# First stage of a conditioned decoder block on one core: both token halves in one loop over eight feature blocks, the modulation 128 columns at a time, three column blocks multiplied behind the loop

## The chip, the core and the metric

The kernel runs on one core of one Trainium2 chip. The metric is the time of one execution on the device in microseconds (us). The engines of the core have these names: PE multiplies matrices (its weight loads are shown as PEld), DVE and ACT work element by element on tiles, POOL is the general engine, SP issues most of the DMA transfers. Every engine works through its own list of instructions in order, so an instruction that waits holds up all that stand behind it in that list, DMA issues included.

## The reference

The block takes 1024 tokens of 1024 features and a conditioning vector `c`. All is float32. Only the first lines bear on the change; the rest (state-space branch, attention, merge, feed-forward) is the same in both kernels.

```python
cond = jax.nn.silu(c)
mod = (cond @ w_ada[l] + b_ada[l])[:, None, :]
sh1, sc1, g1, sh2, sc2, g2 = jnp.split(mod, N_ADA, axis=-1)
h = modulate(rmsnorm(x, norm1_g[l]), sh1, sc1)        # h * (1 + sc1) + sh1
proj = h @ w_in[l]
u, q, k, v, gate_a, gate_b = jnp.split(proj, IN_SPLITS, axis=-1)
y_a = s5_branch(u, ...) @ w_a[l]
y_b = stick_breaking_attention(q, k, v) @ w_b[l]
```

The first stage computes `sh1` and `sc1` (columns 0 to 2047 of `cond @ w_ada`), normalizes and modulates the tokens, keeps `h` turned (features on the partitions) for all later products, and multiplies it with the first 512 columns of `w_in`, which gives `u`, the input of the state-space branch (called S5 here).

## The kernel before

Every float32 product is made as three matmuls of rounded parts: an operand is split into an upper part `h` (a cast, by ACT) and a lower part `l` (the operand less its upper part, by DVE), and upper times upper, upper times lower and lower times upper are added in PSUM. `PRODUCTS` lists the three pairs.

`start` (L563) is the first stage. There the order on every engine is the order of the code (`manual_schedule`). The 1024 tokens are two halves of 512, h = 0 and 1, with four tiles `x` of 128 tokens each; the 1024 features are eight blocks k of 128. The steps are:

- `load(h)` fetches four tiles `x`; `square`, `rstd` and `scale` normalize them in place (the squares' sums are split between ACT and DVE, and so is the scaling).
- `ada_load(g)` fetches the columns of `w_ada` for two feature blocks (256 columns of shift, 256 of scale, four tiles of 512 KB each), g = 0 to 3. `ada_products(g)` multiplies them with `cond` (16 matmuls), ACT copies the result to the tile `acc`, and `ada_sums(g)` adds it up over the partitions with four narrow matmuls. DVE makes `mod` and `G` from it.
- `u_load(a)` fetches the weights of `u` for the feature blocks 2a and 2a+1, and `u_split(a)` makes their upper and lower parts. The four pairs of tiles are called `wh`/`wl` (a = 0 and a = 1, two buffers), `wgh`/`wgl` (a = 2) and `u3h`/`u3l` (a = 3).
- `turn(h, k)` transposes feature block k of a half on PE, and `modulate(h, k)` makes the upper and lower parts of `h` from it, with the steps `hf` (ACT or DVE), cast (ACT, L657) and difference (DVE, L658). They lie in tiles `pa` for half 0 and `pb` for half 1, and are kept for the whole first part of the kernel.
- `product(h, ks, ms)` multiplies feature blocks ks with the column blocks ms (four of 128 columns each), accumulating over all eight k in one PSUM bank for each column block; `store(h, m)` copies a bank to SBUF and writes it to `uD` in memory.
- `idle(n)` issues transposes whose result nobody reads.

First comes a loop over g with half 0 alone, whose second half-tiles `x` are loaded at g = 0 and squared at g = 2; then half 1 in a loop over k. Pieces of `s5.steps` (coefficients of the state-space branch, small DVE operations), `s5.load`, `s5.turned` and `s5.matrices` are called in between.

What follows `start` is put in order by the scheduler: the runs of the S5 branch and `v_proj` (L776), the value projection, whose weights come through `weight` (L438) in the ring of tiles `wh`/`wl`, `wh`/`wl`, `wgh`/`wgl`. So the first two sets of `v_proj` take the tiles in which the weights of `u` for a = 0 (`wh`/`wl`) and a = 2 (`wgh`/`wgl`) lay: a cast into one waits for the last matmul that reads it. A matmul of `v_proj` has 256 columns, and 24 of them on `wh`/`wl` and 24 on `wgh`/`wgl` belong to two token tiles. PE's order of both programs is the same from about 1,300 instructions on.

Of the kernel before, what the change touches and what calls it, by code (L numbers as in the profile page):

```python
# [9 lines left out]
F32 = mybir.dt.float32  # L10
# [18 lines left out]
class S5:  # L29
# [23 lines left out]
    def vexp(self, dst, x, tmp):  # L53
# [8 lines left out]
        v.scalar_tensor_tensor(f, n, -LN2L, f, ALU.mult, ALU.add)  # L62
        v.tensor_scalar(q, f, 1.0 / math.factorial(8), None, ALU.mult)
# [19 lines left out]
    def steps(self):  # L83
# [5 lines left out]
        self.vexp(dt, ldt, tmp)  # L89
# [3 lines left out]
        self.vexp(r, ar, tmp)  # L93
# [336 lines left out]
class Block:  # L430
# [123 lines left out]
    def small(self, const, pp):  # L554

        nc, rows = self.nc, self.rows_
        nc.vector.tensor_copy(rows[0:16].rearrange("p (a b) -> p a b", a=2), self.ld.unsqueeze(2).broadcast_to([16, 2, 64]))
        self.cols = const.tile([P, P], F32, name="cols")
        ps = pp.tile([P, 512], F32, name="mm")
        nc.tensor.transpose(ps[:, 0:P], rows, self.ident)  # L560
        nc.vector.tensor_copy(self.cols, ps[:, 0:P])

    def start(self, const, up, s5p):  # L563
# [5 lines left out]
        w_v = i["w_ada"].rearrange("o (p k) n -> (o p) k n", k=KT)  # L569
        u_v = i["w_in"][0].rearrange("(k p) n -> p k n", p=P)  # L570
        self.hT = [[self.PA.tile([P, 2, 512], F32R, name="pa") for _ in range(KT)], []]
        with self.pool("s0", 1, side="right") as sp, self.pool("s0a", 1, side="right") as ap, self.pool("s5t", 1, side="right") as st, \
                self.pool("s0p", 1, PSUM) as pp, self.pool("s0t", 2, PSUM) as tp, self.pool("s0x", 1, PSUM) as xp, self.pool("s0m", 2, PSUM) as mp, \
                self.tc.manual_schedule(engines={E.PE, E.Activation, E.DVE, E.Pool, E.SP}):
            x = [None] * KT
            ps = pp.tile([P, 2, KT], F32, name="adap")
# [3 lines left out]

# [13 lines left out]
            def u_split(a):  # L594
                w, h, l = us[a]
                nc.scalar.copy(h, w)
                nc.vector.tensor_tensor(l, w, h.bitcast(F32), ALU.subtract)
                ws[a] = self.w3((h, l), 512)

            def ada_load(g):  # L600
                ada[g] = []
                for q in range(2):
                    for a in range(2):
                        w = self.PB.tile([P, 4, 256], F32, name="pb")
                        n = 1024 * q + 256 * g
                        self.last_ada = nc.sync.dma_start(out=w, in_=w_v[:, 4 * a:4 * a + 4, n:n + 256])
                        ada[g].append(w)

            def ada_products(g):
                t = xp.tile([P, 512], F32, name="mm")  # L610
                for q in range(2):
                    for k in range(KT):
                        self.ada_mm(t[:, 256 * q:256 * q + 256], k, ada[g][2 * q + k // 4][:, k % 4])
                ada[g] = ap.tile([P, 512], F32, name="acc", bufs=2)
                nc.scalar.copy(ada[g], t)

            def ada_sums(g):
                for q in range(2):
                    for j in range(2):
                        c = 256 * q + P * j  # L620
                        nc.tensor.matmul(ps[:, q, 2 * g + j:2 * g + j + 1], lhsT=ada[g][:, c:c + P], rhs=self.ones[:, 0:1], start=True, stop=True)
                s = slice(2 * g, 2 * g + 2)
                b = self.cols[:, 64:80].rearrange("p (q k) -> p q k", q=2)
                nc.vector.tensor_tensor(mod[:, :, s], ps[:, :, s], b[:, :, s], ALU.add)
                nc.vector.scalar_tensor_tensor(G[:, s], mod[:, 1, s], 1.0, self.cols[:, 48 + 2 * g:50 + 2 * g], ALU.add, ALU.mult)

            def square(t, act):
                sq = ap.tile([P, 1024], F32, name="sqa" if act else "sqv")
# [5 lines left out]
            def scale(r, t):  # L634
                if t % 4 == 0:
                    nc.scalar.mul(x[t], x[t], r[:, t % 4:t % 4 + 1])
                else:
                    nc.vector.tensor_scalar(x[t], x[t], r[:, t % 4:t % 4 + 1], None, ALU.mult)

            def idle(n):  # L640
                for _ in range(n):
                    nc.tensor.transpose(acc[3][:, 0:P], self.ident, self.ident)
# [6 lines left out]
            def modulate(h, k):  # L649
                t, q = self.hT[h][k], turned[h, k]  # L650
                f = ap.tile([P, 512], F32, name="hf", bufs=2)
                if h == 0 and k % 2 == 0:
                    nc.scalar.activation(t[:, 0], q, AF.Identity, bias=mod[:, 0, k:k + 1], scale=G[:, k:k + 1])
                    nc.vector.tensor_scalar(f, q, G[:, k:k + 1], mod[:, 0, k:k + 1], ALU.mult, ALU.add)
                else:
                    nc.scalar.activation(f, q, AF.Identity, bias=mod[:, 0, k:k + 1], scale=G[:, k:k + 1])
                    nc.scalar.copy(t[:, 0], f)  # L657
                nc.vector.tensor_tensor(t[:, 1], f, t[:, 0].bitcast(F32), ALU.subtract)  # L658

            def product(h, ks, ms):  # L660
                for k in ks:
                    for m in ms:
                        for n, (a, b) in enumerate(((0, 0), (1, 0), (0, 1))):
                            nc.tensor.matmul(acc[m], lhsT=ws[k // 2][a][:, k % 2, P * m:P * m + P], rhs=self.hT[h][k][:, b], start=k + n == 0, stop=k + n == KT + 1)  # L664

            def store(h, m):
                u = up.tile([P, 8, 64], F32, name="us", bufs=4)
                self.upin = (nc.vector.tensor_copy if m % 2 > h else nc.scalar.copy)(u, acc[m].rearrange("p (c j) -> p j c", j=8))
# [10 lines left out]
            acc = [(self.mm, mp)[m // 2].tile([P, 512], F32, name="mm") for m in range(4)]  # L679
# [4 lines left out]
            for t in range(4):  # L684
                scale(r, t)
            turn(0, 0)
            turn(0, 1)
            u_split(0)
            self.small(const, xp)
            ada_products(0)  # L690
# [3 lines left out]
            idle(4)  # L694
            ada_sums(0)
            idle(9)
            for g in range(4):
                k = 2 * g
                modulate(0, k)
# [918 lines left out]
```

## Time and profile before

| what | value |
|---|---|
| median of 3 runs | 1432.78 us (1430.53 to 1435.14) |
| the profiled execution | 1436.13 us |
| its span, first to last instruction | 1434.4 us |
| clock granted to PE, mean | 0.996 |
| PE / DVE / ACT / POOL busy | 98% / 75% / 45% / 36% |
| last matmul of the first stage ends | 93.40 us from the span's start |

The span is cut into what each engine did; a row of the time line gives the start, the length, the engine, the line of the kernel and the tiles (written <- read), and in brackets how long the engine stood still before it and which instruction it waited for. A matmul of 512 columns is recorded with 0.39 to 0.40 us, though the next one starts 0.23 us after it: they overlap in PE's pipeline. The chain of waits is the path that ended last, followed back from the end.

### The profile page before, as it was taken

What the parts mean: (1) busy time and instruction counts of PE and PEld (TensorE: products, weight loads), DVE (VectorE), ACT (ScalarE), POOL (GpSimd) and SP (SyncE); (2) the same over time, 40 slices, a digit from 0 to 9 for tenths busy, and PEclk for the clock granted to TensorE, in tenths of its full rate; (3) what the DMA queues carried; (4) which work ended last, traced back from release to release, by engine and by line L of the source; (5) the groups of instructions that cost most, each with busy time, mean ns of one, the idle gap of its engine ahead of it and who ended that gap; (6) DMA issues with size and microseconds to landing.
All of it is one profiled execution on the core that took longest, in us unless ns stands there. A gap on an engine that the chain in (4) does not pass through costs nothing.

```text
span 1434.4 us, 18472 instructions
## 1 busy us (share of the span) xinstructions
PE 1408.1 (98%) x6821; PEld 1121.3 (78%) x6821; DVE 1078.4 (75%) x1388; ACT 639.9 (45%) x852; POOL 514.5 (36%) x288
## 2 busy tenths in 40 slices
PE   8899999998999999999999999999999999999997
PEld 6689888887666666668888888888888888788886
DVE  5679985656897989877824697877667667799896
ACT  4433324423777776774328442332323233433335
POOL 1020000102101111104400017776767666699394
PEclk9999999999999999999999999999999999999999
DMA  9656667299011112217533234444444359899722
GB/s 338 170 136 178 161 161 213 69 334 310 16 52 52 44 30 81 66 38 240 190 121 118 68 91 152 167 139 162 140 162 138 117 198 386 287 370 364 253 81 117
DMA packets 193274, 233.41 MB, mean 163 GB/s; under 512 B 29468, under 2 KB 128864, under 8 KB 193184
## 3 DMA queue, kind: packets, MB, share of 16 engines
q1 hardware_dynamic: 184048, 224.70, 47.8%
q10 hardware_dynamic: 8912, 7.48, 1.9%
q8 instruction: 54, 0.88, 0.3%
q14 instruction: 36, 0.29, 0.1%
q0 software_dynamic: 224, 0.05, 0.0%
HBM read 162.85 MB, written 68.16 MB: 161 GB/s over the span
## 4 chain that ended last, share of the span: by engine, by line
PE 80%; DVE 9%; DMA 5%; ACT 3%; issue 2%; POOL 1%; SPq 0%; ACTq 0%; POOLq 0%; DVEq 0%
PE tq L1308 12%; PE wo L1308 6%; PE tq L1429 6%; PE mm L1308 6%; PE mx L838 5%; PE mm L838 5%; PE mm L767 4%; PE mm L1429 3%; PE mx L767 3%; PE wo L1429 3%; PE acc L838 2%; PE wo L1145 2%; PE mm L1145 2%; PE mm L664 2%; PE z L838 2%
## 5 line engine op out<-in xcount | busy, mean ns | idle before, releaser
L475 POOL TENSOR_TENSOR ws<-wb 128x1024 f32<-128x1024 f32 x24 | 60.6, 2526 | 171.4 <-DVE wl L478 142.7
L459 POOL TENSOR_TENSOR wl<-ws,wh 128x1024 fp32r<-128x1024 f32 x12 | 31.4, 2616 | 151.4 <-ACT wh L456 150.9
L949 DVE TENSOR_TENSOR wa<-wa,acc 128x512 f32<-128x512 f32 (+1 forms) x80 | 47.0, 628 | 31.0 <-ACT row L947 28.8
L1355 POOL TENSOR_TENSOR pa<-pa 128x512 f32<-128x512 f32 x30 | 63.3, 2136 | 0.3
L1299 POOL TENSOR_TENSOR f<-f,f 128x512 f32<-128x512 f32 x30 | 53.1, 1795 | 26.1 <-DVE f L1293 18.9
L921 ACT ACTIVATE ws<-wa 128x1024 f32<-128x1024 f32 (+1 forms) x40 | 39.0, 976 | 47.6 <-DVE wa L918 47.2
L926 DVE TENSOR_TENSOR wl<-ws,wh 128x1024 fp32r<-128x1024 f32 (+1 forms) x40 | 56.3, 1407 | 1.0
L478 DVE TENSOR_TENSOR wl<-ws,wh 128x1024 fp32r<-128x1024 f32 x23 | 40.8, 1775 | 19.2 <-ACT wh L477 19.1
L1030 DVE SCALAR_TENSOR_TENSOR acc<-aw,cond,acc 128x512 f32<-128x512 f32 x56 | 45.7, 817 | 9.1 <-DMA aw<-in_w_ada_dram 8.4
L1384 POOL TENSOR_TENSOR pa<-pa,row 128x1024 f32<-128x1024 f32 x14 | 43.7, 3135 | 15.5 <-DMA pa<-in_w_ffn_down_dram 15.5
L924 DVE SCALAR_TENSOR_TENSOR ws<-wa,ws 128x1024 f32<-128x1024 f32 (+1 forms) x40 | 45.5, 1137 | 4.3 <-ACT ws L923 3.4
L1292 ACT ACTIVATE f<-f 128x1024 f32<-128x1024 f32 x20 | 21.2, 1061 | 60.6 <-DVE f L1330 31.4
L952 ACT ACTIVATE wa<-wa 128x1024 f32<-128x1024 f32 (+1 forms) x40 | 38.8, 971 | 19.7 <-DVE wa L949 18.7
L838 PE MATMUL z<-q,k 64*128 64x512 f32 (+3 forms) x192 | 41.8, 527 | 4.4 <-DVE na L1095 2.6
L477 ACT CAST wh<-ws 128x1024 fp32r<-128x1024 f32 x23 | 24.2, 1054 | 49.1 <-PE wo L1308 15.5
L456 ACT CAST wh<-ws 128x1024 fp32r<-128x1024 f32 x24 | 25.1, 1048 | 44.2 <-PE wo L1145 21.1
L458 POOL TENSOR_SCALAR wh<-ws 128x1024 fp32r<-128x1024 f32 x6 | 7.2, 1205 | 103.5 <-issue 36.1
L477 ACT CAST wh<-wb 128x1024 fp32r<-128x1024 f32 x25 | 26.2, 1051 | 40.4 <-PE mm L1429 9.7
L475 POOL TENSOR_TENSOR wgs<-wb 128x1024 f32<-128x1024 f32 x12 | 28.9, 2407 | 41.4 <-DVE wl L478 20.3
L1429 PE MATMUL tq<-f,f 128*128 128x512 f32 x136 | 41.7, 389 | 0.0
L838 PE MATMUL mm<-wa,V 128*64 128x512 f32 (+3 forms) x192 | 39.8, 507 | 0.0
L478 DVE TENSOR_TENSOR wl<-wb,wh 128x1024 fp32r<-128x1024 f32 x25 | 38.3, 1536 | 1.9 <-ACT wh L477 1.9
(849 smaller groups left out, 4701.6 us busy)
## 6 DMA issues: line engine op xcount, KB each, us to landing
wb<-hD SPq DMA_DIRECT2D x40, 512.0 KB, 5.6
aw<-in_w_ada_dram SPq DMA_DIRECT2D x64, 256.0 KB, 4.4
hD<-f SPq DMA_DIRECT2D x30, 512.0 KB, 5.1
ws<-in_w_in_dram SPq DMA_DIRECT2D x23, 512.0 KB, 4.6
wb<-in_w_ffn_gate_dram SPq DMA_DIRECT2D x44, 256.0 KB, 4.4
wb<-in_w_ffn_up_dram SPq DMA_DIRECT2D x44, 256.0 KB, 4.8
ws<-hD SPq DMA_DIRECT2D x20, 512.0 KB, 6.0
x<-in_x_dram SPq DMA_DIRECT2D x16, 512.0 KB, 7.4
```

What stands on the lines that cost most here:

```text
L475: (add or nc.gpsimd).tensor_tensor(st, a, b, op)
L477: nc.scalar.copy(h, a)
L478: self.last_lo = (lo or nc.vector).tensor_tensor(l, a, h.bitcast(F32), ALU.subtract)
L767: self.nc.tensor.matmul(ps, lhsT=w[a][:, k], rhs=act[h][k][:, b], start=(j == 0), stop=(j == n - 1))
L838: return self.tc.keep_in_program_order(self.nc.tensor.matmul(*args, **kw))
L926: nc.vector.tensor_tensor(lt, st, ht.bitcast(F32), ALU.subtract)
L949: nc.vector.tensor_tensor(a[:, x, 0:f], a[:, x, 0:f], r[:, x, 0:f], ALU.subtract)
L1145: self.nc.tensor.matmul(ps, lhsT=mg[t // 4][k][:, a, P * (t % 4):P * (t % 4) + P], rhs=ws[k // 2][b][:, k % 2], start=k + j == 0, stop=k + ...
L1299: self.last_sum = nc.gpsimd.tensor_tensor(o, a, b, op)
L1308: self.nc.tensor.matmul(ps, lhsT=w[x][:, q, k], rhs=self.B[i](y, k), start=(j == 0), stop=(j == 11))
L1355: self.after(nc.gpsimd.tensor_tensor(t[:, n], part(a), part(b), SIGN_B[i]), first)
L1429: nc.tensor.matmul(ps, lhsT=o[x][:, P * t:P * t + P], rhs=o[y][:, R], start=(j == 0), stop=(j == 3 * np_ - 1))
```

## The change

The columns of `w_ada` are fetched and multiplied for one feature block at a time (eight blocks, tiles `[P, 4, 2, P]`, four transfers of 256 KB with rows of 512 bytes in place of two transfers of 512 KB with rows of 1 KB for the same block); the products' bank and the sums' bank become one. The second half of `x` is loaded behind the second block. One loop over k = 2 to 7 does both halves. Five of the eight column blocks, (0,0), (0,1), (0,2), (1,0) and (1,1) as (half, column block), accumulate in the loop; (0,3), (1,2) and (1,3) follow behind it, feature blocks 6 and 7 first and then 0 to 5. The squares are written into tiles `pa` that are still empty, the scaling of half 1 is cut into 256 and 768 columns, `modulate` makes `hf` always on ACT and has three buffers for it, and `vexp` of the S5 coefficients is cut in two. `idle` is called with 78, 3 and 14 where it was 78, 4 and 9. The number of products (192 of 512 columns), of ada matmuls (64), sums (16) and used transposes (64) stays.

```diff
-            def ada_load(g):
-                ada[g] = []
-                for q in range(2):
-                    for a in range(2):
-                        w = self.PB.tile([P, 4, 256], F32, name="pb")
-                        self.last_ada = nc.sync.dma_start(out=w, in_=w_v[:, 4 * a:4 * a + 4, n:n + 256])
+            def ada_load(k):
+                ada[k] = []
+                for a in range(2):
+                    w = (ap.tile([P, 4, 2, P], F32, name="ada", bufs=4) if k in (3, 5, 6, 7) else self.PB.tile([P, 4, 2, P], F32, name="pb"))
+                    for q in range(2):
+                        self.last_ada = nc.sync.dma_start(out=w[:, :, q], in_=w_v[:, q, 4 * a:4 * a + 4, P * k:P * k + P])
...
+            def ada_products(k):
+                for n in range(KT):
+                    self.ada_mm(sums[:, 0:256], n, ada[k][n // 4][:, n % 4].rearrange("p q n -> p (q n)"))
+                ada[k] = ap.tile([P, 256], F32, name="acc", bufs=2)
+                nc.scalar.copy(ada[k], sums[:, 0:256])
...
-                f = ap.tile([P, 512], F32, name="hf", bufs=2)
-                if h == 0 and k % 2 == 0:
+                f = ap.tile([P, 512], F32, name="hf", bufs=3)
+                if direct:
                     nc.scalar.activation(t[:, 0], q, AF.Identity, bias=mod[:, 0, k:k + 1], scale=G[:, k:k + 1])
-                    nc.vector.tensor_scalar(f, q, G[:, k:k + 1], mod[:, 0, k:k + 1], ALU.mult, ALU.add)
-                else:
-                    nc.scalar.activation(f, q, AF.Identity, bias=mod[:, 0, k:k + 1], scale=G[:, k:k + 1])
+                nc.scalar.activation(f, q, AF.Identity, bias=mod[:, 0, k:k + 1], scale=G[:, k:k + 1])
+                if not direct:
                     nc.scalar.copy(t[:, 0], f)
...
+            late = (0, 3), (1, 2), (1, 3)
...
             load(0)
+            ada_load(0)
             u_load(0)
-            ada_load(0)
+            ada_load(1)
+            load(1)
             u_load(1)
-            ada_load(1)
+            ada_load(2)
+            ada_load(3)
+            u_load(2)
+            ada_load(4)
+            u_load(3)
+            ada_load(5)
...
+            for cs in (first, rest):
+                for t in range(4, 8):
+                    scale(r, t, cs)
+                if cs == first:
+                    idle(14)
+                    for k in range(2):
+                        turn(1, k)
+                        modulate(1, k)
+            u_high(1)
+            u_low(1)
+            ada_products(2)
+            turn(0, 2)
+            product(1, (0,), (0, 1))
+            ada_sums(2)
+            modulate(0, 2)
+            ada_products(3)
...
+            for k in range(2, 8):
+                product(0, (k,), (0,))
+                if k < 7:
+                    ada_sums(k + 1)
+                next(steps)
+                if k < 7:
+                    modulate(0, k + 1)
+                product(0, (k,), (1, 2))
...
+                turn(1, k)
+                modulate(1, k)
+                if k > 2:
+                    product(1, (k - 1,), (0, 1))
+                if k in (3, 5):
+                    u_high(k // 2 + 1)
+                    u_low(k // 2 + 1)
+                if k < 6:
+                    ada_products(k + 2)
+                    turn(0, k + 2)
...
+            product(0, (6, 7), (3,))
+            product(1, (7,), (0, 1))
+            for m in range(2):
+                store(1, m)
+            product(1, (6, 7), (2, 3))
...
+            product(0, range(6), (3,))
...
+            s5.matrices()
+            product(1, range(6), (2,))
+            store(1, 2)
+            product(1, range(6), (3,))
+            store(1, 3)
```

Three places of the engines' lists show how the instructions move. A row gives line, operation, tile written <- tiles read, and its size; a number behind it counts equal rows in sequence.

**PE, end of the first stage.** Before, the last column block of half 1 (on `u3h`/`u3l`) stands among the first matmuls of `v_proj`, L788:

```order
L788 MATMUL mm<-wgh,pa 128x256 x2
L221 MATMUL tp<-ident,dsk 16x32
L664 MATMUL mm<-pb,u3h 128x512
L664 MATMUL mm<-pb,u3l 128x512
L664 MATMUL mm<-pb,u3h 128x512 x2
L664 MATMUL mm<-pb,u3l 128x512
```

Now the last products read `wh`/`wl` (feature blocks 0 to 3) and `wgh`/`wgl` (4 and 5), and `v_proj` (L817 now) starts behind all of them:

```order
L662 MATMUL mm<-pb,wh 128x512 x2
L662 MATMUL mm<-pb,wl 128x512
L662 MATMUL mm<-pb,wgh 128x512 x2
L662 MATMUL mm<-pb,wgl 128x512
L662 MATMUL mm<-pb,wgh 128x512 x2
L662 MATMUL mm<-pb,wgl 128x512
L817 MATMUL mm<-wh,pa 128x256 x2
L817 MATMUL mm<-wl,pa 128x256
```

The 48 matmuls of `v_proj` on `wh`/`wl` now come first, then four on `wgh`, and the fifth of that set reads `wgl`; before, 22 matmuls of `v_proj`, some on `wgl` already, stood ahead of the first stage's last twelve.

**DVE, the same place.** Before, the lower part `wgl` of the second set of `v_proj` is made in the middle of the S5 coefficients, still in the first stage:

```order
L161 TENSOR_TENSOR tmp<-tmp,cols 128x16
L162 TENSOR_TENSOR tmp<-lpi,cols 128x16
L459 TENSOR_TENSOR wgl<-wgs,wgh 128x1024
L163 TENSOR_TENSOR tmp<-tmp 128x16
L164 TENSOR_TENSOR tmp<-tmp 128x16
```

Now it stands behind the S5 operations that follow the first stage (`e`, `tc`, `o`, `scr`) and behind the first step of a later stage's modulation (`acc<-aw`, L1057):

```order
L281 TENSOR_TENSOR o<-C,A 128x576 x2
L280 TENSOR_TENSOR scr<-Cs,B 128x576 x2
L78 TENSOR_TENSOR e<-e,p_1090 128x4x32
L79 TENSOR_TENSOR e<-e,p_1091 128x4x32
L76 TENSOR_TENSOR tc<-tc,wr 128x16x4
L1057 TENSOR_SCALAR acc<-aw,cond 128x512
L74 TENSOR_TENSOR y<-tn,wi 128x16x4
L75 TENSOR_TENSOR h<-tc,wi 128x16x4
L77 TENSOR_TENSOR tn<-tn,wr 128x16x4
L282 TENSOR_TENSOR o<-o,scr 128x576
L460 TENSOR_TENSOR wgl<-wgs,wgh 128x1024
```

The split of `wgl` moved back by some thirty rows, past all of these; the split of `wl` stands 31 rows ahead of it.

**ACT, early in the first stage.** Before, the copy `acc` of an ada product stands behind the cast of the next weights:

```order
L653 ACTIVATE pa<-tp,mod_141,G_142 128x512
L656 ACTIVATE hf<-tp,mod_141,G_142 128x512
L657 CAST pa<-hf 128x512
L596 CAST wh<-ws 128x1024
L615 COPY acc<-mm 128x512
```

Now that of feature block 2 stands behind two modulations of half 1, the rest of a tile's scaling and the cast of the second weights:

```order
L653 ACTIVATE hf<-tp,mod_138,G_139 128x512
L655 CAST pb<-hf 128x512
L653 ACTIVATE hf<-tp,mod_138,G_139 128x512
L655 CAST pb<-hf 128x512
L633 ACTIVATE x<-x,ry 128x768
L595 CAST wh<-ws 128x1024
L614 COPY acc<-sums 128x256
```

The copy, on which the next narrow sums wait, had half 0's modulation and one cast of weights ahead of it; now two modulations of half 1, the rest of a scaling and that cast stand ahead of it.

More of the change, by code (lines that the diff above doesn't have):

```diff
@@ L558, in small @@
         self.cols = const.tile([P, P], F32, name="cols")
[L559 to L561 removed]
+        nc.tensor.transpose(pp[:, 0:P], rows, self.ident)
+        nc.vector.tensor_copy(self.cols, pp[:, 0:P])
     def start(self, const, up, s5p):
@@ L609, in ada_products @@
-            def ada_products(g):
-                t = xp.tile([P, 512], F32, name="mm")
-                for q in range(2):
[L612 to L622, printed above, removed]
+            def ada_load(k):
[4 more added lines that the diff above has]
+                        self.last_ada = nc.sync.dma_start(out=w[:, :, q], in_=w_v[:, q, 4 * a:4 * a + 4, P * k:P * k + P])
+                    ada[k].append(w)
@@ L623, in ada_sums @@
                 b = self.cols[:, 64:80].rearrange("p (q k) -> p q k", q=2)
                 nc.vector.tensor_tensor(mod[:, :, s], ps[:, :, s], b[:, :, s], ALU.add)
-                nc.vector.scalar_tensor_tensor(G[:, s], mod[:, 1, s], 1.0, self.cols[:, 48 + 2 * g:50 + 2 * g], ALU.add, ALU.mult)
+                nc.vector.scalar_tensor_tensor(G[:, s], mod[:, 1, s], 1.0, self.cols[:, 48 + k:49 + k], ALU.add, ALU.mult)
             def square(t, act):
-                sq = ap.tile([P, 1024], F32, name="sqa" if act else "sqv")
+                sq = self.hT[0][4 + t % 4].rearrange("p a b -> p (a b)")
@@ L743, in start @@
-            for k in range(6):
-                turn(1, k + 2)
-                product(1, (k,), range(4))
-                modulate(1, k + 2)
-                if k < 3 or k == 5:
-                    next(steps)
-            s5.matrices()
-            for m in range(4):
-                product(1, (6, 7), (m,))
-                store(1, m)
-                if m == 1:
-                    s5.turned()
+            for n in range(3):
+                for m in range(3):
+                    multiply(0, 0, m, n)
+                if n == 0:
+                    ada_sums(1)
+                    modulate(0, 1)
@@ new lines, in start @@
+            product(0, (1,), (0, 1, 2))
+            for t in range(4, 8):
+                square(t, t % 2 == 0)
+            r = self.rstd(const, ss[:, 4:8], 4)
+            for cs in (first, rest):
[8 more added lines that the diff above has]
+            u_low(1)
@@ new lines, in start @@
+            ada_products(2)
[4 more added lines that the diff above has]
+            ada_products(3)
+            ada_load(6)
+            turn(0, 3)
+            product(1, (1,), (0, 1))
+            for k in range(2, 8):
[6 more added lines that the diff above has]
+                product(0, (k,), (1, 2))
+                if k == 7:
+                    for m in range(3):
+                        store(0, m)
+                turn(1, k)
[8 more added lines that the diff above has]
+                    turn(0, k + 2)
+                if k == 3:
+                    ada_load(7)
+                if k == 4:
+                    s5.load()
@@ new lines, in start @@
+            for (h, m), p in zip(late, (self.mm, self.mm, mp)):
+                acc[h, m] = p.tile([P, 512], F32, name="mm")
+            product(0, (6, 7), (3,))
[3 more added lines that the diff above has]
+            product(1, (6, 7), (2, 3))
+            s5.turned()
+            next(steps)
+            product(0, range(6), (3,))
+            next(steps)
+            next(steps)
+            store(0, 3)
+            next(steps)
+            s5.matrices()
```

107 lines of the change are left out of this document (37 added, 70 removed).

## The prediction, made before the changed kernel had run

> **What bounds the kernel now.** I read the page's list of engines first, then PE's time line of the first stage, its windows at the largest gap, the chain of waits, and last the rows of ACT, DVE and the DMA around both ends of the stage.
>
> ```profile
> PE 1408.1 (98%) x6821; PEld 1121.3 (78%) x6821; DVE 1078.4 (75%) x1388; ACT 639.9 (45%) x852; POOL 514.5 (36%) x288
> ```
>
> PE is busy for 98% of the span. The change leaves the count of its matmuls alone, so it can win only where PE stands still or runs slowly. PE's time line has these gaps in the first stage:
>
> ```profile
> 13.64 0.60 PE L647 MATMUL tp<-ident,x 128*128 128x128 f32 x3 [0.17 <-ACT x L636]
> 14.57 0.77 PE L647 MATMUL tp<-ident,x 128*128 128x128 f32 x5 [0.33 <-DVE x L638]
> 15.97 0.33 PE L560 MATMUL mm<-ident,rows 128*128 128x128 f32 x1 [0.63 <-DVE rows L557]
> 16.68 1.93 PE L1015 MATMUL mm<-pb,cond 128*32 128x256 f32 x32 [0.38 <-DVE cols L561]
> 21.63 0.50 PE L664 MATMUL mm<-pa,wh 128*128 128x512 f32 x1 [0.22 <-ACT pa L653]
> 23.21 0.74 PE L664 MATMUL mm<-pa,wh 128*128 128x512 f32 x2 [0.84 <-DVE pa L658]
> ...
> 47.99 1.05 PE L621 MATMUL adap<-ones,acc 128*128 128x1 f32 x8 [0.68 <-ACT acc L615]
> ...
> 54.08 0.50 PE L664 MATMUL mm<-pa,u3h 128*128 128x512 f32 x1 [2.19 <-ACT pa L653]
> 54.42 0.40 PE L664 MATMUL mm<-pa,u3l 128*128 128x512 f32 x1
> 55.65 1.22 PE L664 MATMUL mm<-pa,u3h 128*128 128x512 f32 x2 [0.84 <-DVE pa L658]
> ```
>
> The brackets sum to 6.28 us. A recorded operation overlaps the next one, so each gap costs more than its bracket: a matmul is recorded with 0.40 (the row at 54.42) and at full clock followed after 0.23 (below), which is 0.17 more for each of nine gaps. That makes **7.8 us** of standing still. The clock granted to PE (the number ahead of the DMA share) falls in the last of them:
>
> ```profile
> 54.00:55.00 1.00, 0.73 (x2) 0.30 (x2) 0.90 (x2) 0.97 (x3) 0.00 (x0) 0.90 0.57 192
> 55.00:56.00 1.00, 0.35 (x1) 0.35 (x2) 1.00 (x2) 1.00 (x2) 0.00 (x0) 0.50 0.02 6
> 61.00:62.00 1.00, 1.00 (x7) 0.80 (x6) 0.00 (x0) 0.40 (x1) 0.00 (x0) 0.69 0.00 0
> 62.00:63.00 1.00, 1.00 (x6) 0.82 (x6) 0.00 (x0) 0.97 (x3) 0.00 (x0) 1.00 0.00 0
> ```
>
> The chain of waits shows what that costs, and how the stage ends:
>
> ```profile
> 55.65 5.91 PE mm L664 x13
> ...
> 71.46 2.78 PE mm L664 x12
> ...
> 87.58 2.70 PE mm L788 x22
> 90.40 3.00 PE mm L664 x12
> 93.40 3.10 PE mm L788 x26
> 96.50 5.76 PE mx L788 x48
> ```
>
> Twelve matmuls at full clock take 2.78 (0.23 each), thirteen after the gap 5.91 where 3.0 would do: **2.9 us** for the half clock. The stage thus loses 10.7 us. Its last matmul ends at 93.40, with 22 matmuls of `v_proj` (2.70) drawn ahead of it; without them the stage ends at 90.7. Behind it PE runs `v_proj` without a gap at 0.12 for each matmul (48 in 5.76).
>
> **The first stage after the change.** Durations of the steps come from the groups by form; rstd's length from DVE's time line.
>
> ```profile
> L656 ACT ACTIVATE hf<-tp,mod,G 128x512 f32<-128x512 f32 x12 | 9.3, 775 | 4.3 <-DVE sa L115 1.5 <-DVE pb L658 1.5 <-PE tp L647 1.3
> L657 ACT CAST pa<-hf 128x512 fp32r<-128x512 f32 x4 | 2.5, 620 | 0.1
> L658 DVE TENSOR_TENSOR pa<-hf,pa 128x512 fp32r<-128x512 f32 x8 | 5.2, 688 | 0.1
> L596 ACT CAST wh<-ws 128x1024 fp32r<-128x1024 f32 x2 | 2.1, 1040 | 0.0
> L792 ACT COPY vst<-mx 128x256 f32<-128x256 f32 x4 | 1.5, 372 | 9.1 <-DMA vD<-vst 6.7 <-PE mx L788 2.4
> L636 ACT ACTIVATE x<-x,ry 128x1024 f32<-128x1024 f32 x2 | 2.3, 1150 | 0.8 <-DVE ry L491 0.8
> L624 DVE TENSOR_TENSOR mod<-adap,cols 128x4 f32<-128x4 f32 x4 | 0.6, 158 | 4.8 <-PE adap L621 4.8
> ...
> 9.62 1.23 DVE L632 SCALAR_TENSOR_TENSOR sqv<-x 128x1024 f32<-128x1024 f32 x1 [1.74 <-DMA x<-in_x_dram]
> ...
> 10.96 0.17 DVE L485 TENSOR_SCALAR rv<-ss 128x4 f32<-128x4 f32 x1
> ...
> 12.44 2.08 DVE L638 TENSOR_SCALAR x<-x,ry 128x1024 f32<-128x1024 f32 x3
> ```
>
> And the DMA rates (last number, GB/s), first for rows of 4 KB, then for the ada tiles' rows of 1 KB, and at 457 us for rows of 512 bytes (columns of `w_in`, 128 wide, as the new ada tiles are):
>
> ```profile
> 32.00:33.00 1.00, 1.00 (x6) 0.84 (x5) 0.93 (x2) 0.38 (x2) 0.00 (x0) 1.00 1.04 418
> 39.00:40.00 1.00, 1.00 (x6) 0.83 (x5) 0.27 (x3) 0.60 (x1) 0.00 (x0) 1.00 1.09 348
> 457.50:458.00 0.50, 0.50 (x5) 0.13 (x2) 0.50 (x1) 0.50 (x3) 0.00 (x0) 1.00 1.15 350
> 458.00:458.50 0.50, 0.50 (x3) 0.41 (x4) 0.47 (x2) 0.50 (x2) 0.00 (x0) 1.00 1.03 311
> ```
>
> I take 320 GB/s for the narrow rows, near the lower of the two windows, and keep 250 and 350 as ends; 250 is an estimate, as far below 311 again as 311 is below 350, and half as much more.
>
> The new waits of PE, in order:
>
> 1. The first two transposes' gaps stay: 0.5 in brackets, **0.8** as above.
> 2. Block 1 of `w_ada` follows x's first half, block 0 and the first u weights: 1.05 + 1.05 MB at 320 and 0.52 MB at 418 take 7.8 us from 9.62, so it lands at 17.5 to 18.4 (the upper end with 290 GB/s and the small loads between). PE's second run of transposes starts at 14.57 as before; the rest of them, eight ada matmuls (half of 1.93), eight more transposes and idle ones and two sums bring it to about 17.2: **0.9**, for a landing at 18.1.
> 3. Sums of block 1, then `mod` and `G` (0.16 each, as in the row of `mod`), `hf` 0.78, cast 0.62, difference 0.69 stand before block 1's products, and PE has only six matmuls (1.4) beside them: **1.1** in two pieces, where the same place cost 0.22 + 0.84.
> 4. x's second half (2.1 MB at 418, 5.0 us) lands at 23 to 23.5. The last square (1.34, from 9.62 to 10.96 the first time), rstd (1.48, 10.96 to 12.44) and 256 columns of scaling give 27 to 28; PE's products end at 24.9, and 14 idle transposes cover 1.5: **1.1**.
> 5. Behind it the lower part of the first half-1 block: **0.3**.
> 6. The copy `acc` of block 2 stands on ACT behind two modulations of half 1 (2 × 1.40), 768 columns of scaling (0.9 of 1.15) and a cast of 1.04, and takes 0.37: with the first transposed block at 28.1 it ends at 33.2. PE has the transposes, eight ada matmuls and six products to do and asks for it at 31.7: **1.5**.
> 7. In the loop: 0.4 at the first modulation, 0.5 each where the lower halves of the weights of blocks 4 and 6 come late: **1.4**.
>
> Together **7.1**. Inside the loop the chain from sums to the cast and difference is 0.32 + 0.78 + 0.62 + 0.69 and some semaphore time, 2.8 in all; PE has 3.2 to 4.7 us of products of the other half and ada work beside it, so it is hidden; the cover gone, each block would cost up to 2.8. The gap of 2.19 goes because no S5 step stands ahead of six `mod`s in one; what is late next there are item 7's halves. The four more idle transposes (0.11 each) and some more changes between kinds of matmul cost 0.5. The split scaling and the squares' new place are off the path but for item 4. No single gap of the loop is near 2.19, so I drop the half clock there: 7.8 + 2.9 − 7.1 − 0.5 = **3.1 us gained**, and the stage's last matmul ends at E = 87.6 (against 90.7). At 350 GB/s it is 0.7 earlier, at 250 GB/s some 1.5 later (items 2 and 4).
>
> The Trainium skill, page "DMA: Bandwidth & Descriptors", section "Specifications", puts the smallest transfer for full rate at 512 bytes; by it the new rows would cost nothing against 1 KB. The 350 and 311 agree only in part, and 418 for 4 KB rows speaks against a single limit there. By that rule E would be at the early end, 86.9.
>
> **The hand-over to `v_proj`.** This is where the change takes something back.
>
> ```profile
> 85.03 1.23 DVE L459 TENSOR_TENSOR wgl<-wgs,wgh 128x1024 fp32r<-128x1024 f32 x1 [0.19 <-ACT wgh L456]
> ...
> 93.48 0.07 DVE L230 MEMSET tc<- 128x16 f32 x1 [4.20 <-PE mm L664]
> ...
> 101.84 0.18 DVE L78 TENSOR_TENSOR tn<-tn,h 128x32 f32<-128x32 f32 x1
> 103.18 0.49 DVE L1028 TENSOR_SCALAR acc<-aw,cond 128x512 f32<-128x512 f32 x1 [1.15 <-DMA aw<-in_w_ada_dram]
> ```
>
> Before, both weight sets of `v_proj` were split in the first stage, at no cost. Now the late blocks read u's `wh`/`wl` until twelve matmuls before the end (E − 2.8), and `wgh`/`wgl` until E. The first set: cast 1.04, difference 1.23 (DVE idle there, as in the 4.20 before 93.48), ready at E − 0.2; no wait. The second set's cast comes after E, behind five u loads that ACT issues; its difference is on DVE behind the S5 work that took from 93.48 to 102.0 before, of which 8.3 stand between the two differences (rows of `o`, `scr`, `e`, and the step `acc<-aw`; a few rows before and behind). So `wgl` is ready at E − 0.2 + 8.3 + 1.23 = E + 9.3, say 9.4. PE has 48 matmuls on the first set (5.76) and four on `wgh` (0.5) and is empty at E + 6.3. **A wait of 3.1 us.** Its ends: nothing, if the S5 rows run shorter or wait less than they did; 4.5, if the `aw` load is late by its 1.15 again, since DVE waits in order. Behind the waiting matmul on PE stand 43 others of the same two token tiles, and the S5 runs behind these; nothing else can run.
>
> A gap of 2.19 and 0.84 halved the clock. This one is as long in one piece. I take it that the clock halves, at 2.9 before; here matmuls of 256 columns run behind it, and I put **2.5** (ends 0 and 2.9).
>
> Afterwards, an estimate by DVE's later rows and their group means, the next weights of `v_proj` are split some 0.6 us before PE needs them, 36 us after E: no wait, with little to spare. PE then runs without a gap to 347 as before, in the same order. There it waits for a chain fed by DMA, which moves with PE's own earlier work:
>
> ```profile
> 349.97 0.93 PE L838 MATMUL z<-q,k 64*128 64x128 f32 x8 [2.58 <-DVE na L1095]
> ```
>
> If that chain stands still while PE shifts, up to 2.58 us of a loss is swallowed there, and a gain is lost; I keep it as a pull toward zero.
>
> **The sum.** −3.1 + 3.1 + 2.5 = +2.5 us. The profiled execution took 1436.13 (span 1434.4 and 1.7 around it), 3.35 above the median of the three; it would become 1438.6. Against the median, 1432.78 + 2.5 = **1435.3**.
>
> **The rivals.**
>
> *The clock holds at the hand-over.* The half clock of before followed two gaps close together and a microsecond with PE busy 0.35; one wait of 3.1 between full stretches may be too little, or the later chain swallows part. Then −3.1 + 3.1 = 0: 1432.8. For it: the gap of 0.84 at 23.21 left the clock whole. Against it: 3.1 is more than 2.19 and 0.84 together. The Trainium skill, page "TensorE: Matmul & The Clock Gate", section "Why this matters for your kernels", allows gaps of up to about 3 us between bursts; by that rule 2.19 should not have halved the clock, and the trace disagrees, while 3.1 sits on the rule's edge.
>
> *No wait at the hand-over.* If the S5 rows on DVE run sooner than PE's last products (they need only the coefficients, and E moves), `wgl` is ready before E + 6.3. Then only the gain is left: −3.1, 1429.7, at best −4.6 with rows at 350 and some of item 7 gone. Against it: `tc` waited for PE's last product before, and the rows are placed behind `wl`, which waits for PE until E − 2.8.
>
> *Slower: the early waits grow into a half clock.* Items 2 to 6 lie between 17 and 33 us, five waits with 4.9 us in 16. If narrow rows move below 270 GB/s, item 2 or 4 grows past the 2.19 that sufficed before; the waits add 1.5 and the clock 2.9 more. That is +2.5 + 4.4 = +6.9: 1439.7.
>
> **How the numbers follow.** The forecast gets 0.40, the holding clock 0.24, no wait 0.17, the slower case 0.19. The range reaches from the fast end of "no wait" (1428) to the slow case with a wait of 4.5 (1441). A measurement of this kernel can tell about 0.3%, 4.3 us, from no change. Faster by more needs "no wait" and fast rows: 0.12. Slower by more takes most of the slow case and the upper end of the forecast (a wait of 4.5): 0.22. The rest, 0.66, lies within.
>
> **What would show it.** PE's time line must have no gap of 2 us and full clock at 50 to 60; the last product near 88; gaps of about 0.9 to 1.5 at ada block 1, at the first transposes of half 1 and at the sums of block 2; and one gap near 94 that waits for DVE's `wgl`, with the clock at 0.50 behind it. I am wrong if ada tiles end waits inside the loop, if `wgl` is split before E + 6, or if a new wait stands between 100 and 347.

## The result, and the profile after

| what | before | after |
|---|---|---|
| median of the timed runs | 1432.49 us (4 runs) | 1440.53 us (4 runs) |
| profiled execution / span | 1436.13 / 1434.4 | 1439.84 / 1438.1 |
| a second profiled execution / span | 1432.84 / 1431.1 | 1440.29 / 1438.6 |

The ratio is 1.0056 (95% interval 1.0044 to 1.0068): the change makes the kernel 8 us slower. The second profiles are two of the experiments (e7 and e8), and they matter: before's first profile was an execution 3.6 us above this median.

PE's time line of the changed kernel, its rows with a wait of 0.2 or more up to 110 us (without the start, where PE waits 2.62), and the first row of `v_proj`:

```profile
13.42 0.60 PE L644 MATMUL tp<-ident,x 128*128 128x128 f32 x3 [0.65 <-ACT x L633]
14.36 0.33 PE L644 MATMUL tp<-ident,x 128*128 128x128 f32 x1 [0.34 <-DVE x L635]
17.36 1.36 PE L1044 MATMUL sums<-pb,cond 128*32 128x256 f32 x16 [0.31 <-DVE mod L621]
21.93 0.50 PE L662 MATMUL mm<-pa,wh 128*128 128x512 f32 x1 [0.48 <-ACT pa L655]
22.66 0.50 PE L662 MATMUL mm<-pa,wh 128*128 128x512 f32 x1 [0.23 <-DVE pa L656]
27.63 1.14 PE L644 MATMUL tp<-ident,x 128*128 128x128 f32 x8 [1.32 <-ACT x L633]
33.22 0.61 PE L618 MATMUL sums<-ones,acc 128*128 128x1 f32 x4 [1.21 <-ACT acc L614]
34.70 1.07 PE L1044 MATMUL sums<-ada,cond 128*32 128x256 f32 x16 [0.88 <-DVE mod L621]
49.01 0.50 PE L662 MATMUL mm<-pa,wgl 128*128 128x512 f32 x1 [0.28 <-DVE wgl L599]
61.44 0.50 PE L662 MATMUL mm<-pa,u3l 128*128 128x512 f32 x1 [0.28 <-DVE u3l L599]
76.23 0.19 PE L222 MATMUL tp<-ident,dsk 32*16 32x32 f32 x1 [0.24 <-ACT C L219]
...
88.73 0.40 PE L817 MATMUL mm<-wh,pa 128*128 128x256 f32 x2
...
98.78 0.58 PE L817 MATMUL mm<-wgl,pa 128*128 128x256 f32 x1 [3.65 <-DVE wgl L460]
```

The loop itself does what it says: from 36 us to the end of the stage no wait reaches 0.3. `v_proj` starts at 88.73, and the last product of the first stage is recorded to 88.89 (before to 93.40, or 90.70 without the 2.70 of `v_proj` drawn ahead of it). Then comes the one large gap, 3.65 us, and it waits for `wgl`. DVE's time line shows the two differences, wl and wgl, ten us apart; ACT's shows the cast that wgl needs behind five loads of u, which ACT issues (ACTq is its DMA queue):

```profile
87.07 1.26 DVE L460 TENSOR_TENSOR wl<-ws,wh 128x1024 fp32r<-128x1024 f32 x1
...
97.50 1.22 DVE L460 TENSOR_TENSOR wgl<-wgs,wgh 128x1024 fp32r<-128x1024 f32 x1
```

```profile
89.03 4.08 ACTq L314 DMA_DIRECT2D u<-uD  x5
93.14 1.06 ACT L457 CAST wgh<-wgs 128x1024 fp32r<-128x1024 f32 x1 [3.57 <-DMA u<-uD]
```

The cast ended at 94.20. DVE took up the difference only at 97.50, with S5 rows without a pause ahead of it. The windows (the number ahead of the DMA share is PE's granted clock) show the price behind the gap:

```profile
90.00:92.00 2.00, 2.00 (x19) 2.00 (x18) 2.00 (x8) 0.00 (x0) 1.84 (x4) 1.00 1.23 140
...
96.00:98.00 2.00, 0.00 (x0) 0.00 (x0) 2.00 (x7) 0.00 (x0) 0.00 (x0) 0.94 1.03 131
98.00:100.00 2.00, 1.22 (x5) 1.23 (x6) 2.00 (x5) 0.00 (x0) 0.00 (x0) 0.50 1.01 316
102.00:104.00 2.00, 2.00 (x11) 2.00 (x11) 2.00 (x6) 0.13 (x1) 0.00 (x0) 0.50 0.56 132
104.00:106.00 2.00, 2.00 (x17) 2.00 (x16) 0.94 (x5) 0.62 (x2) 0.00 (x0) 0.86 0.98 309
```

The window from 102 to 104, at half clock, counts eleven matmuls in 2 us; the one from 90 to 92, at full clock, counts nineteen. The chain has "98.78 5.06 PE mm L817 x22" where 22 matmuls took 2.70 before. At the far end of the stretch that PE alone sets stands the first `z`, for the changed kernel and for before's second profile:

```profile
353.07 0.93 PE L867 MATMUL z<-q,k 64*128 64x128 f32 x8 [0.84 <-DVE na L1124]
```

```profile
347.81 0.93 PE L838 MATMUL z<-q,k 64*128 64x128 f32 x8 [1.50 <-DVE na L1095]
```

These rows give a ruler for everything below. E is the recorded end of the first stage's last product (in before and its variants less the 2.70 of `v_proj` drawn ahead of it), Z the time at which PE is ready for `z` (the row's start less its wait). Z − E holds the same work in every kernel:

| profile | E | Z − E | wait at z | first z | span | median, us |
|---|---|---|---|---|---|---|
| before | 90.70 | 256.69 | 2.58 | 349.97 | 1434.4 | 1432.2 to 1432.8 |
| before, second (e7) | 89.63 | 256.68 | 1.50 | 347.81 | 1431.1 | |
| after | 88.89 | 263.34 | 0.84 | 353.07 | 1438.1 | 1440.5 |
| after, second (e8) | 88.71 | 263.35 | 2.10 | 354.16 | 1438.6 | |
| e1 own tiles | 92.53 | 263.90 | 2.41 | 358.84 | 1440.5 | 1444.0 |
| e2 gap filled | 90.25 | 260.94 | 0.84 | 352.03 | 1436.7 | 1440.1 |
| e3 before, gap filled | 87.67 | 256.68 | 4.04 | 348.39 | 1434.0 | 1432.5 |
| e4 before, narrow rows | 93.93 | 256.67 | 1.56 | 352.16 | 1435.0 | 1437.5 |
| e5 late order | 88.87 | 265.91 | 2.61 | 357.39 | 1441.3 | 1442.4 |
| e6 late order, earlier copy | 88.39 | 265.08 | 1.10 | 354.57 | 1438.0 | 1439.8 |
| e9 the same, token pairs | 88.33 | 257.84 | 3.29 | 349.46 | 1434.7 | 1435.8 |
| e9 again (e12) | 88.34 | 259.33 | 1.31 | 348.98 | 1433.0 | |
| e10 wgl on POOL | 90.56 | 265.16 | 1.14 | 356.86 | 1441.2 | 1440.9 |

In before Z − E is the same in four profiles of three kernels, to 0.02. The change adds 6.65 to it: 3.65 of wait, 0.16 of pipeline behind it (a matmul of 256 columns is recorded with 0.28 and followed after 0.12), and 2.84 that remain for the half clock and what goes with it; the 22 matmuls of the chain alone took 2.36 longer. Of the second profiles, 7.5 us apart in span, 6.7 is this, −0.9 the earlier E, 0.6 the wait at `z`, and 1.1 lies behind `z`, where the profiles of all kernels scatter by some 4 us from first z to the end (1082 to 1086).

### The profile page after: what moved, and what is told of

It reads as the page before. It is cut to its first block, busy times and chain, and to the rows that moved or that the text cites. A ratio compares the mean times of both kernels' runs of the same rounds, so it can differ in the third digit from the quotient of the medians.

```text
span 1438.1 us, 18524 instructions
## 1 busy us (share of the span) xinstructions
PE 1409.4 (98%) x6825; PEld 1120.6 (78%) x6825; DVE 1079.6 (75%) x1397; ACT 642.7 (45%) x859; POOL 515.5 (36%) x288
## 4 chain that ended last, share of the span: by engine, by line
PE 81%; DVE 9%; ACT 3%; DMA 2%; issue 2%; POOL 1%; SPq 1%; ACTq 0%; POOLq 0%; DVEq 0%
PE tq L1337 12%; PE wo L1337 6%; PE tq L1458 6%; PE mm L1337 6%; PE mx L867 5%; PE mm L867 5%; PE ga L796 5%; PE mm L796 4%; PE mm L1458 3%; PE mx L796 3%; PE wo L1458 3%; PE acc L867 2%; PE wo L1174 2%; PE mm L1174 2%; PE mm L662 2%; PE z L867 2%
## 5 line engine op out<-in xcount | busy, mean ns | idle before, releaser
L478 ACT CAST wh<-ws 128x1024 fp32r<-128x1024 f32 x23 | 24.1, 1054 | 49.4 <-PE wo L1337 15.4
```

The source lines that it names most:

```text
L478: nc.scalar.copy(h, a)
```

## The experiments

**Taking the hold away by tiles (e1).** The third pair of u weights gets tiles of its own; room comes from fewer buffers elsewhere.

```diff
-ring = self.wring[a] if a < 3 else (ap, "u3h", "u3l", self.wring[0][3], "ws", 2)
+ring = self.wring[a] if a < 2 else (ap, f"u{a}h", f"u{a}l", *((self.wring[2][3], "wgs", 1) if a == 2 else (self.wring[0][3], "ws", 2)))
-f = ap.tile([P, 512], F32, name="hf", bufs=3)
+f = ap.tile([P, 512], F32, name="hf", bufs=2)
-w = (ap.tile([P, 4, 2, P], F32, name="ada", bufs=4) if k in (3, 5, 6, 7) else self.PB.tile([P, 4, 2, P], F32, name="pb"))
+w = (ap.tile([P, 4, 2, P], F32, name="ada", bufs=3) if k in (3, 5, 6, 7) else self.PB.tile([P, 4, 2, P], F32, name="pb"))
```

> The changed kernel with tiles of their own for the third pair of u weights (u2h, u2l), so that no late product holds the tiles of the second v_proj set; two buffers fewer (hf 3 to 2, ada 4 to 3) make room. Theory (the loss is the hand-over: a wait of 3.65 for wgl and a half clock behind it worth 2.65): neither appears, the time falls by 6.3, from 1440.5 to about 1434.2. Rival (the loss lies elsewhere, in the early waits or in a later stage): the gap near 95 goes, but the time stays above 1437.

1444.0 us, ratio to before 1.0080 (1.0067 to 1.0092), slower than the change. The gap near 95 was gone, but the smaller `hf` ring opened two others in the stage (0.70 and 0.84 near 69, with half clock to 74; E 92.53), and PE waited 4.48 at 131.53 for the difference of a later weight set. Neither theory had that. It was no clean test, since the buffers were cut with it.

**Filling the gap (e2)** puts 32 matmuls of 256 columns, into unused columns of the same bank, where PE waits.

```diff
 for a, b in PRODUCTS:
+    if (c, t, k, a, b) == (0, 0, 4, 0, 1):
+        for _ in range(32):
+            nc.tensor.matmul(ps[:, 256:512], lhsT=self.hT[0][0][:, 0, 0:P], rhs=ws[0][0][:, 0], start=False, stop=False)
     nc.tensor.matmul(ps[:, 0:256], lhsT=self.hT[t // 4][k][:, a, P * (t % 4):P * (t % 4) + P],
                      rhs=ws[k // 4][b][:, k % 4], start=(j == 0), stop=(j == 23))
```

> The changed kernel with 32 matmuls of 256 columns, whose result nobody reads, on PE in the place of the wait at the hand-over (3.7 us of work for a wait of 3.65). The wait is not removed, only filled. Theory (the half clock behind the gap is a price of its own): the clock stays at 1.00 from 95 to 106 and the time falls by 2.65, to about 1437.9. Rival (the half clock costs nothing on the path, something later sets the end): no change, 1440.5.

No gap, full clock there, and Z − E fell by 2.4, of the 2.65 expected: the half clock is a price of its own on PE's path to `z`. The time hardly moved, 1440.1 (1.0055, 1.0041 to 1.0068), as the rival had it. In this profile the clock had halved elsewhere, behind the early waits (0.61 in the window from 36 to 40), and E was 1.4 later than in the change, so that PE was ready for `z` only 1.0 earlier. The same happened in e10, and in no other of the nine profiles that have these waits. But this profile is the fastest of the five runs (1438.4), so that early half clock does not explain why the others took 1439.2 to 1441.3. Why the gain does not reach the time stays open.

**Filling before's gap (e3).**

```diff
...
+            for _ in range(22):
+                nc.tensor.transpose(adap[:, 256:384], self.ident, self.ident)
-            product(0, (6,), range(4))
+            product(0, (6,), (0,))
+            product(0, (6,), range(1, 4))
```

> The kernel before with 22 transposes on PE, whose result nobody reads, in the gap at 51.8 us (2.4 us of work for a gap of 2.19). In the profile the clock stays at 1.00 from 54 to 62 and the first stage ends 2.9 earlier. If the timed runs of before lose the clock there as the profiled run did: 2.9 faster than before, 1429.6. If they mostly do not (which would explain why before's profiled execution is 3.6 slower than its median, while the changed kernel's is 0.7 faster than its own): no change within 1, about 1432.

The clock stayed whole from 54 to 62 and E came 3.0 (first profile) or 2.0 (second) earlier. The time is that of before, 0.9996 (0.9984 to 1.0009). Its first `z` shows where the gain went:

```profile
348.39 1.65 PE L842 MATMUL z<-q,k 64*128 64x128 f32 x8 [4.04 <-DVE na L1099]
```

PE was ready at 344.35, 2 to 3 us earlier than before, and waited 4.04 instead of 1.50 or 2.58. The chain that releases `z` (`na`, fed by DMA from some 300 us on) did not move with PE. Behind this gap the clock was 0.50 from 348 to 354, so a part was lost once more. This profile is also the slowest of its eleven runs (1435.8, median 1432.5), so how long the usual run waits there is not shown.

**Narrow rows alone (e4):** before, each load of `w_ada` cut in two.

```diff
-self.last_ada = nc.sync.dma_start(out=w, in_=w_v[:, 4 * a:4 * a + 4, n:n + 256])
+for j in range(2):
+    self.last_ada = nc.sync.dma_start(out=w[:, :, P * j:P * j + P], in_=w_v[:, 4 * a:4 * a + 4, n + P * j:n + P * j + P])
```

> The kernel before with each load of w_ada cut into two of 128 columns, so rows of 512 bytes, nothing else. The last u weights land at 45.35 in before, behind 8.4 MB of these rows. At 320 GB/s against 348 they land 2.1 later and the gap of 2.19 grows by 1 to 2: about 1434. At 250 GB/s they land 9 later: about 1440. At 350 GB/s: no change.

1437.5, ratio 1.0038 (1.0026 to 1.0051): 4.8 slower, between the cases. The cast of the last u weights, which waits for their landing, in before and here:

```profile
45.37 1.05 ACT L596 CAST u3h<-ws 128x1024 fp32r<-128x1024 f32 x1 [3.87 <-DMA ws<-in_w_in_dram]
```

```profile
49.83 1.05 ACT L596 CAST u3h<-ws 128x1024 fp32r<-128x1024 f32 x1 [4.91 <-DMA ws<-in_w_in_dram]
```

4.5 us later for 8.4 MB of narrow rows; 24.1 us at 348 GB/s become 28.6, about 294 GB/s (an estimate from these two rows). The changed kernel's windows have the same rate (last number) where it loads `w_ada`, less than the 320 of the forecast:

```profile
26.00:28.00 2.00, 0.68 (x6) 0.40 (x5) 1.54 (x7) 0.71 (x3) 0.00 (x0) 1.00 1.20 291
28.00:30.00 2.00, 1.94 (x24) 0.91 (x22) 0.17 (x1) 1.60 (x3) 0.00 (x0) 1.00 1.17 290
```

Yet none of its waits names an `ada` load; its second profile has one, of 0.16. Narrow rows are slow, and the new loop, which needs a block only at its turn, hides that.

**Late products in another order (e5),** the clean form of e1: same matmuls and buffers, and the third pair of weights is read first. The flag that ends each sum moves with the order.

```diff
-product(1, range(6), (2,))
+product(1, (0, 1), (2, 3))
+product(1, (4, 5), (2, 3))
+product(1, (2, 3), (2,))
 store(1, 2)
-product(1, range(6), (3,))
+product(1, (2, 3), (3,))
 store(1, 3)
```

> The changed kernel with the last products of half 1 in another order: feature blocks 0, 1 and 4, 5 of both late column blocks first, 2 and 3 (on the second pair of u weights, which v_proj does not need at first) last. Same matmuls, same buffers. Both sets of v_proj are then free 2.8 us or more before the stage ends, and DVE has both differences ahead of the S5 rows. Theory (the loss is the hand-over): no gap and no half clock near 95; 3.65 + 0.17 + 2.65 = 6.5 less up to the wait at 350, and about 1434 in time, less if the DMA chain at 350 swallows a part as it did with the filled gap of before (there 1.5 of 3.0). Rival (the rest of the change costs as much): above 1437.

1442.4 (1.0066, 1.0054 to 1.0079). The gap at the hand-over was gone, as the theory has it, and still nothing was won:

```profile
128.01 0.58 PE L819 MATMUL mm<-wl,pa 128*128 128x256 f32 x1 [5.08 <-DVE wl L460]
```

PE used the two sets up without a wait and stood before the next one: its `wl` now stood on DVE behind the widest S5 rows (four of 128x1024 at 1.2 us each), and the clock halved behind it. This was not foreseen; my theory of one wait at one place fell, and was replaced: the scheduler has S5 rows and weight differences in one DVE list, and whichever difference comes free late is put behind a block of S5 rows (`wgl` in the change, `wl` in e1 and here).

**An earlier copy (e6):** as e5, with `u_high(1)` and `u_low(1)` behind `ada_sums(2)` and `modulate(0, 2)`.

> As the run before, and the cast and difference of the second u weights stand behind the sums and the modulation of block 2, so that the copy of block 2 (ACT) and its mod (DVE) come earlier. The gaps of 1.21 (sums wait for the copy) and 0.88 (the next ada products wait for mod, since products and sums share a bank) should go: 2.4 us earlier at the end of the first stage. Theory: 2.4 less than the run before if the later chain lets it through, 1431.6. Rival (the wait at 350 takes what is gained ahead of it): within 1 of the run before.

1439.8 (1.0050, 1.0037 to 1.0064). The wait of 1.21 fell to 0.27, that of 0.88 to 0.69, a new one of 0.42 came; E moved by only 0.5. The wait near 128 was 5.47. The time fell by the 2.4 that was expected, and a little more (2.6 against e5), but not by the expected way: of the 3.3 between the profiles' spans, 0.5 is the earlier E, 0.8 lies between E and Z, 1.5 is a shorter wait at `z`, and 0.5 lies behind it.

**Second looks at both kernels (e7, e8).**

> The kernel before, unchanged, for a second profile. If its first profile was an execution slower than usual (1436.1 against a median of 1432.7), this one shows where: theory, a half clock of some 7 us in another place or in none, worth up to 2.9, and a shorter or longer wait at 350; the rival is that the places are the same and the difference lies in the DMA stretch from 290 to 350.

> The changed kernel, unchanged, for a second profile. The wait for wgl and the half clock behind it should be there again, with 3.6 and 2.6, since they hang on the order of the lists. If the half clock is a matter of chance it may be missing.

Before's second profile took 1432.84, its median. The same gaps are there, with the same 2.19, but the clock was below full only from 56 to 60, and the thirteen matmuls behind them took 1.08 less; the wait at `z` was 1.08 shorter. The changed kernel's second profile repeats the first: 3.65 for `wgl`, half clock to 105.

**Token tiles in pairs (e9, e12):** as e6, and `v_proj` makes all 48 matmuls of two token tiles on its first set, then all 48 on the second.

```diff
-for t in range(KT):
-    ps = self.mm.tile([P, 512], F32, name="mm")
-    for k in range(KT):
+for t0 in range(0, KT, 2):
+    pss = [self.mm.tile([P, 512], F32, name="mm") for _ in range(2)]
+    for half in range(2):
+        for t, ps in zip((t0, t0 + 1), pss):
+            for k in range(4 * half, 4 * half + 4):
...
```

> As the last run but one (free order), and v_proj takes two token tiles together: all 48 matmuls on its first weight set, then all 48 on the second, so that the first set's tiles come free 5.8 us before PE needs the next weights, and the list of DVE has that difference (wl) ahead of the wide S5 rows instead of behind them. Theory (what is lost is where the lists put the weights' differences between S5 rows, first wgl at the hand-over, then wl at 128): no gap near 95 and none near 128, PE is at the first z 256.7 us after the stage's end, as in before, and the time is 1431 to 1433. Rival (DVE has no room for S5 and the differences, a gap opens elsewhere): again a wait of 3 us or more before 347, and 1438 or more.

> The run with token tiles in pairs once more, for a second profile. Its first showed PE at the first z 346.2 us after the start, as early as before (346.3 and 347.4), but a wait of 3.3 there and half clock behind it. If the chain that releases z (DVE and DMA, from 290 on) is what is late, the wait is again 2 us or more and the first z starts at 348 to 350; if it was chance, the wait is 1.5 and the time about 1433.

Between 77 and 200 us PE had no wait of 0.2 or more in the first profile (1.35 and 0.25 in the second), and Z − E was 257.8, within 1.2 of before. 1435.8, ratio 1.0021 (1.0011 to 1.0032): 4.7 less than the change, where e6, the same without the pairs, had 0.8 less, so the lists' order is what costs. But it is still slower than before, and than the 1431 to 1433 expected. PE was ready for `z` at 346.17, as in before, and waited 3.29 there, with the clock at 0.50 behind it from 349 to 355; the second time at 347.67, with 1.31. Its `z` starts at 349 both times, 1.2 to 1.7 later than in before's usual profile. Why `na` is late there isn't settled.

**The difference on POOL (e10).** `lo_eng=nc.gpsimd` for the second set of `v_proj`.

> The changed kernel with the difference wgl of the second v_proj set made by POOL (2.6 us there, but POOL is idle) instead of DVE, so it follows the cast at once. The wait of 3.65 falls to about 1.8. Theory: the gap costs 1.8 less, and if a gap of 1.8 in one piece leaves the clock whole, the half clock (2.65) goes too: about 1436; if the clock halves all the same, 1438.7. Rival (the next differences on DVE become the bound, as in the run with the late products in another order): a new gap near 128 and 1440 or more.

1440.9 (1.0059, 1.0045 to 1.0073). The wait grew to 6.18, against both expectations: POOL was not idle but slow.

```profile
91.23 4.54 POOL L207 TENSOR_SCALAR B<-lpi 64x144 f32<-64x144 f32 x1
...
99.95 2.96 POOL L460 TENSOR_TENSOR wgl<-wgs,wgh 128x1024 fp32r<-128x1024 f32 x1
```

**The hold in the kernel before (e11):** the tiles of the third and fourth pair of u weights exchanged, so that before's last products hold `wgh`/`wgl`.

```diff
-ring = self.wring[a] if a < 3 else (ap, "u3h", "u3l", self.wring[0][3], "ws", 2)
+own, held = (ap, "u3h", "u3l"), self.wring[2][0:3]
+ring = self.wring[a] if a < 2 else (*own, *self.wring[2][3:]) if a == 2 else (*held, self.wring[0][3], "ws", 2)
```

> The kernel before with the tiles of the third and the fourth pair of u weights exchanged (u3h/u3l for feature blocks 4 and 5, wgh/wgl for 6 and 7), nothing else: the last products of before then hold the tiles of the second v_proj set, as the late blocks of the changed kernel do. In the lists wgl moves behind the S5 rows on DVE. Theory (holding these tiles to the end is enough, without the new loop): a wait of 2 to 4 for wgl near 100 and a half clock behind it, PE at the first z 4 to 7 us later than in before, and 1437 to 1439. Rival (the hold costs only together with the shorter first stage or the eight feature blocks): no wait over 1, 1432 to 1434.

1439.6, ratio 1.0043 (1.0026 to 1.0060), 6 to 7 us, from an exchange of names. PE was ready for `z` at 352.93, 5.5 to 6.6 later than in before. The waits are not those of the theory, which had one of 2 to 4 for `wgl`: the scheduler moved S5 matmuls into the gap, PE waits for those and for `wgh`, 2.55 in all, and the clock was 0.50 behind the second of them, from 99 to 102.

```profile
96.70 0.50 PE L789 MATMUL mm<-wgh,pa 128*128 128x256 f32 x2 [0.48 <-ACT wgh L456]
98.57 1.85 PE L259 MATMUL s5a<-ident,e 128*128 128x128 f32 x8 [1.12 <-DVE e L77]
106.10 1.70 PE L289 MATMUL s5a<-o,bst 128*16 128x128 f32 x14 [0.95 <-POOL bst L208]
```

So holding these tiles to the stage's end, with what the scheduler then makes of it, is enough for a loss of this size; the new loop isn't needed for it.

## Why the prediction was right, and where its terms were off

The mechanism was the forecast's: the stage gets shorter, the late blocks hold the tiles of `v_proj`'s weights, PE waits for `wgl`, and the clock halves behind the wait. The time lies in the range, near its upper end: +8.0 where +2.5 was forecast. That the range holds it is in part luck. Its upper end was drawn for a wait of 4.5 and a half clock in the loop, and neither came. "Slower by more" than 4.3, which is what was measured, had been given 0.22. By terms:

- *First stage, −3.1.* Measured −1.8 between the first profiles and −0.9 between the second ones. About half of the miss is my baseline: I took 2.9 for the half clock at 55 from one execution, and the second has 1.08 less. The rest is E, 88.89 instead of 87.6. The brackets sum to 6.2, 8.1 with 0.17 each, where I had 7.1. Items 3, 5 and 7 were too high (0.48 + 0.23, no row, 0.28 + 0.28), items 1 (0.65 + 0.34), 4 (1.32) and 6 (1.21) near; item 2 was no DMA wait at all, though its rows moved at 290 GB/s and not at 320. What I missed are two waits for `mod` (0.31 and 0.88): the ada products now share a bank with the sums, and each product waits until DVE has read the sums before it.
- *No half clock in the loop*: right in both profiles of the change. The slower rival's mechanism, half clock from the early waits, did show in two variants (e2, e10), without slower rows.
- *The wait at the hand-over, 3.1*: 3.65. `wgl` was ready at E + 9.8 (98.72), not E + 9.4; nearly all of it is DVE's list, as argued. The u loads on ACT did not set the end (the cast ended 3.3 before the difference began), nor did the `aw` load.
- *The half clock, 2.5*: 2.8 with its surroundings, so the rival of the holding clock fell. By the Trainium skill, page "TensorE: Matmul & The Clock Gate", section "Why this matters for your kernels", gaps over about 3 us cost the clock; 3.65 agrees, while before's 2.19 and 0.84 stay against that figure, now in two profiles.
- *No wait afterwards*: right for the change. e5 and e6 show how thin that was: with `wgl` in time, the next set was late.
- *The pull toward zero at 350*: seen for a gain in the profiles of e3 and e9, not in e12's. For this loss it scatters: in the first profiles the wait fell from 2.58 to 0.84 and took up 1.7, in the second ones it grew from 1.50 to 2.10. The usual before waits 1.50 there, not 2.58, so there was little to swallow.
- *The baseline*, the larger part of the miss. Profile against profile the change cost 3.71 (1439.84 less 1436.13) where +2.5 was forecast: the terms were off by 1.2 together, which would be 2.9 without those 1.7. The other 4.3 of the 8.0 come from moving that difference to the medians: before's profiled execution was 3.64 above its median, the changed kernel's 0.69 below. The prediction named the 3.35 it saw and took it as a constant; e7, at the median, has 1.08 less of half clock and 1.08 less of wait at `z`, so that the usual execution of before has less to gain and less to swallow a loss with.

## What to carry to other kernels

When a loop is rearranged so that its last work reads other tiles, look at who takes those tiles next: what was split at no cost under the old loop may now come behind a full list of another engine, and at 6.7 us it outweighed everything the new loop won. A term read from one profile, a half clock above all, is a sample; take a second profile before a gain is built on it. And a gain ahead of a stretch that another resource sets (here `na` and its DMAs at 350) can show up as a longer wait there.

## What the runs showed of the hardware

- The half clock's length differs between executions with the same gaps: behind 2.19 and 0.84 it lasted from 55 to 61.5 in one profile and from 56 to 59.7 in another. A gap of 1.35 (e12) left the clock whole.
- At the first `z`, behind a long stretch of full work, the gap's length and the clock go together: in the ten profiles with a gap of 0.84 to 2.58 there the clock stayed whole, in the four with 2.61 (e5), 3.10 (e11), 3.29 (e9) and 4.04 (e3) it halved. Shorter gaps that stand close together halved it elsewhere: 2.19 and 0.84 (before), 0.70 and 0.84 (e1), 0.48 and 1.12 (e11).
- The first transposes and ada products, with waits of at most 0.68 between 13 and 17 us, ran at a whole clock in three profiles (before, e7, e11) and at about half from 16 to 20 us in two (e3, e4; mean 0.57). The edit of e3 changes nothing in that stretch.
- One POOL row can take far longer where DVE is busy: the copy `bst` of 64x256 took 0.39 in before, with DVE idle all the while, and 13.85 in e11, where DVE ran without a pause (POOL's time lines, before and e11):

```profile
92.35 0.39 POOL L207 COPY bst<-bbr 64x256 f32<-64x256 f32 x1
```

```profile
91.75 13.85 POOL L207 COPY bst<-bbr 64x256 f32<-64x256 f32 x1
```

  That DVE's work is the cause was not tested, and spans on POOL are rough; but PE's row at 106.10 above waited for the copy behind it.
- Rows of 512 bytes moved at 290 GB/s in the changed kernel's windows, and by the estimate from e4's landing at about 294 over 8.4 MB, against 348 for rows of 1 KB.
